# The folded weights' results go through the raw-weight ring, in stores of 512 KB

## The chip, the cores and the metric

The kernel runs on one core of a Trainium2 chip. A core has a matrix engine (TensorE, PE in the profile), a vector engine (VectorE, DVE), a scalar engine (ScalarE, ACT), GpSimd (POOL) and SyncE (SP), which here only issues DMAs. Each engine takes its instructions in order and waits on semaphores; DMAs are issued from the queues of SP, ACT and POOL. The metric is the time of one execution in microseconds (us), lower is better; a run's time is compared with that of the kernel before on the same chip.

## The reference

A decoder layer over 2048 tokens of width 1024: retention (4 heads) and a pooling mixer beside each other, an output projection, cross-attention into 256 memory tokens, a gated MLP with a short convolution, and a last norm, all in f32. What matters here is the part on the weights:

```python
y_pool = pool_mixer(u, pool_w[l], pool_scale[l])            # per group g: pooled_g @ pool_w[g] * scale
x = x + jnp.concatenate([y_ret, y_pool], axis=-1) @ w_out[l]
...
q = (h @ wq).reshape(B, S, XA_HEADS, XA_HEAD_DIM)
k, v = jnp.split(mem_n @ wkv, 2, axis=-1)
s = jnp.einsum('bshd,bmhd->bhsm', q, k) * (XA_HEAD_DIM ** -0.5)
p = jax.nn.softmax(s, axis=-1)
o = jnp.einsum('bhsm,bmhd->bshd', p, v).reshape(B, S, D_MODEL)
return o @ wo
```

The memory has only 256 rows, so the kernel multiplies weights by it once: M = wq k^T (for the scores straight from the hidden state), VW = v wo (for the output straight from the probabilities), and WP = pool_w w_out (pooled rows straight into the output projection). These are the folded weights.

## The kernel before

Every f32 matrix is split into a high and a low part (`split`, line 230: ACT copies the high part, DVE subtracts for the low part), and a product is three matmuls (`passes`, line 239, lines 241 to 243). `unit` (line 286) multiplies one 1024 x 128 block of a weight with 1024 tokens: 48 matmuls of 128x512 into two PSUM banks.

Raw weights come from memory into `R`, a ring of five places of 512 KB (`raws`, line 145). `new_raw` (line 245) takes the place that was given back first and gives it back at once, so places go around in the order in which the program takes them, whatever order the loads are issued in. A load waits for the last reader of its place. From `R` a unit's weights are split into `Q` (three pairs of halves), the rows of `wqT`, `wo` and `wout_p` into pieces of `G` (`row_pairs`, line 424).

`folded_weights` (line 361) is a generator; its steps are put between the units of the first 1024 tokens. First come the keys and values of the memory (16 steps). Then, from line 461 on, the part of this change:

- M: for each of four heads two row pairs of `wqT`, four PSUM banks of 12 matmuls (128x256) each; a bank is evacuated by ACT in two halves (line 473) and stored in `Md` (256 KB).
- VW: for each head two row pairs of `wo`, four banks of 6 matmuls (128x512), each evacuated by ACT (line 491) and stored in `VWd` (256 KB).
- WP: `poolT` and four row pairs of `wout_p`, eight banks of 3 matmuls, evacuated at line 512 and stored in `WPd`.

The evacuation goes into a temporary (`TT`, ten of 256 KB, shared with retention, pooling and the norms), and `keep` (line 432) issues the store on ACT's own DMA queue and gives the temporary back, to be written again when the store has landed.

The order of the program around it (line 1517): head 0 has its gate, q and k units, with one M step behind q and one behind k; head 1 the same; head 2 has two VW steps behind q and two behind k; head 3 two WP steps behind q and the rest behind k; then come four pool groups. Retention of a head runs in steps between the matmuls of the next units. The order in which each engine issues its instructions is made by a scheduler that works on its own estimate of times, so it may put instructions of neighbouring steps before one another, and it differs between the two kernels in this stage. Weight sums for the MLP (`weight_sums`, line 906) are made by copies on SP (line 916) and accumulating DMAs on POOL (lines 918 to 925) through the same time.

Of the kernel before, what the change touches and what calls it, by code (L numbers as in the profile page):

```python
# [11 lines left out]
AF = mybir.ActivationFunctionType  # L12
# [5 lines left out]
KT = D // P  # L18
SEQ = 2048
NMEM = 256  # L20
T = 1024
SUB = 512
# [97 lines left out]
def trunk(ctx, tc, xT, memT, pos, w_qkgu, w_v, wkv, wqT, wo, wout_r, wout_p, poolT, w_up, w_dn, vecs, consts, outT):  # L120
    nc = tc.nc
    pe, act, dve, pool, sp = nc.tensor, nc.scalar, nc.vector, nc.gpsimd, nc.sync
# [19 lines left out]
    TT = Arena(cp.tile([P, TEMPS * TW], F32, tag="T", name="T"), 0, TEMPS, TW)  # L142
# [9 lines left out]
    def vec(n):  # L152
        nonlocal o
        o += n
        return vc[:, o - n : o]

    mixg, xag, memg, ffng, fing = (vec(KT) for _ in range(5))
# [29 lines left out]
    t = TT.take()  # L187
# [5 lines left out]
    Md = drp.tile([2, KT, P, SUB], F32, tag="Md", name="Md")  # L193
    VWd = drp.tile([KT, P, KT, P], F32, tag="VWd", name="VWd")
    rope_d = drp.tile([2, P, SUB], F32, tag="rope_d", name="rope_d")
    WPd = drp.tile([KT, P, 4, P], F32, tag="WPd", name="WPd")

    def mmps():
        return mmp.tile([P, SUB], F32, tag="mm", name=nm("mm"))
# [30 lines left out]
    def split(src, hi, lo, g=None):  # L230

        if g is None:
            act.activation(hi, src, AF.Copy)  # L233
            tt(dve, lo, src, hi.bitcast(F32), ALU.subtract)
        else:
            act.activation(hi, src, AF.Identity, scale=g)
            stt(lo, src, g, hi.bitcast(F32), ALU.mult, ALU.subtract)

    def passes(ps, lhs, rhs, start, stop, more=False):
        (lh, ll), (rh, rl) = lhs, rhs  # L240
        pe.matmul(ps, lh, rh, start=start, stop=False, skip_group_check=more)  # L241
        pe.matmul(ps, lh, rl, start=False, stop=False, skip_group_check=more)  # L242
        pe.matmul(ps, ll, rh, start=False, stop=stop, skip_group_check=more)  # L243

    def new_raw():
        r = raws.take()
        r.free()
        return r.f
# [112 lines left out]
    def folded_weights():  # L361
# [20 lines left out]
        rn = smp.tile([P, 4], F32, tag="rnm", name="rnm", bufs=1)[:, :2]  # L382
# [17 lines left out]
        def project(n):  # L400

            if n < 2:
                hs = first[0] if n == 0 else pairs(first[1])
            elif n < KT and n % 2:

                z = Z.take()
                hs = pairs(load_tile(wkv[n], z))
                z.free()
            elif n % 2:
                zs = [TT.take() for _ in range(2)]  # L410
                for i in range(2):
                    sp.dma_start(zs[i].f[:, :SUB], wkv[n, :, 4 * i : 4 * i + 4].rearrange("p k n -> p (k n)"))
                hs = pairs([z.f[:, :SUB] for z in zs])
                for z in zs:
                    z.free()
            else:
                hs = pairs(load_tile(wkv[n]))
            ps = mmps()[:, :NMEM]
            for k in range(KT):
                w = [hs[k // 4][:, i, (k % 4) * P : (k % 4 + 1) * P] for i in range(2)]  # L420
                passes(ps, w, (mh[:, k], ml[:, k]), k == 0, k == KT - 1)
            return ps

        def row_pairs(src):
            raw = new_raw()
            sp.dma_start(raw, src)
            u = B.take(2)
            for i in range(2):
                split(raw[:, i * SUB : (i + 1) * SUB], u.r[:, i * SUB : (i + 1) * SUB], u.r[:, T + i * SUB : T + (i + 1) * SUB])
            return u  # L430

        def keep(dst, t, n):
            act.dma_start(dst, t.f[:, :SUB].rearrange("p (n c) -> p n c", n=n))
            t.free()

        def tiles4(d, nh, k):
            return d[4 * nh : 4 * nh + 4, :, k, :].rearrange("n p c -> p n c")

        kk = B.take(4)
        kp4 = kk.r.rearrange("p (n i m) -> p n i m", i=2, m=NMEM)  # L440
# [2 lines left out]
        for n in range(KT):  # L443
            ps = begun[n] if n < 2 else project(n)
            t = TT.take()
# [8 lines left out]
        for n in range(KT):  # L454
            ps = project(KT + n)
# [5 lines left out]
        for h in range(HEADS):  # L461
            dp = [row_pairs(wqT[(2 * h + dt) * P : (2 * h + dt + 1) * P, :]) for dt in range(2)]
            for k2 in range(KT // 2):
                ps = mmps()
                for j in range(2):
                    for dt in range(2):
                        k = 2 * k2 + j
                        w = [dp[dt].r[:, i * T + k * P : i * T + (k + 1) * P] for i in range(2)]
                        passes(ps[:, j * NMEM : (j + 1) * NMEM], w, (kp4[:, 2 * h + dt, 0], kp4[:, 2 * h + dt, 1]), dt == 0, dt == 1)
                t = TT.take()  # L470
                for j in range(2):
                    k = 2 * k2 + j
                    act.activation(t.f[:, j * NMEM : (j + 1) * NMEM], ps[:, j * NMEM : (j + 1) * NMEM], AF.Identity, scale=xag[:, k : k + 1])
                keep(Md[h // 2, 2 * k2 : 2 * k2 + 2, :, (h % 2) * NMEM : (h % 2 + 1) * NMEM].rearrange("k p m -> p k m"), t, 2)
            for u in dp:
                u.free()
            if h == HEADS - 1:
                kk.free()
            yield

        for h in range(HEADS):
            dp = [row_pairs(wo[(2 * h + dt) * P : (2 * h + dt + 1) * P, :]) for dt in range(2)]
            for mt in range(2):
                for nh in range(2):
                    ps = mmps()
                    for dt in range(2):
                        lh = [vp4[:, 2 * h + dt, i, mt * P : (mt + 1) * P] for i in range(2)]
                        w = [dp[dt].r[:, i * T + nh * SUB : i * T + (nh + 1) * SUB] for i in range(2)]
                        passes(ps, lh, w, dt == 0, dt == 1)
                    t = TT.take()  # L490
                    act.activation(t.f[:, :SUB], ps, AF.Identity, scale=rn[:, mt : mt + 1])
                    keep(tiles4(VWd, nh, 2 * h + mt), t, 4)
            for u in dp:
                u.free()
            if h == HEADS - 1:
                vv.free()
            yield
# [6 lines left out]
        split(raw[:, :SUB], pw.r[:, :SUB], pw.r[:, SUB:])  # L504
        for g in range(4):
            u = row_pairs(wout_p[g])
            for nh in range(2):
                ps = mmps()
                lh = [pw.r[:, i * SUB + g * P : i * SUB + (g + 1) * P] for i in range(2)]
                passes(ps, lh, [u.r[:, i * T + nh * SUB : i * T + (nh + 1) * SUB] for i in range(2)], True, True)  # L510
                t = TT.take()
                act.activation(t.f[:, :SUB], ps, AF.Copy)
                keep(tiles4(WPd, nh, g), t, 4)
            u.free()
            if g == 3:
                pw.free()
            yield
# [950 lines left out]
    def later_tiles(b, j, rb):  # L1468
# [11 lines left out]
        after(2, step)  # L1480

    todo = folded_weights()

    def folded(n):
# [14 lines left out]
    for b in range(NB):  # L1499
# [4 lines left out]
        rn, rb, last = normed  # L1504
# [119 lines left out]
    old, TT = TT, Places([], SUB)  # L1624
# [104 lines left out]
```

## Time and profile before

| | |
|---|---|
| median of 3 runs | 2493.02 us (2491.94 to 2494.43) |
| profiled execution | 2497.84 us, span 2495.7 us |
| TensorE busy | 2441.3 us (98%) |
| ACT busy | 1220.2 us (49%) |
| DVE busy | 1704.0 us (68%) |
| mean granted TensorE clock | 0.991 |
| stores of folded weights | 16 to Md, 16 to VWd, 8 to WPd, 256 KB each |
| first and last of them issued | 144.8 us and 337.4 us |

A row of waits reads: who waited, on whom, total us, times, longest. A row of the timeline: start, length, engine, line, operation, what it writes and reads. A row of windows: the stretch, its length, busy time and instruction count of TensorE, its weight loads, DVE, ACT and POOL, the granted TensorE clock (1.00 is full), the DMA engines' busy share, GB/s. A DMA row: what it writes and reads, the issuing queue, count, KB each, us from issue to landing.

### The profile page before, as it was taken

The page shows a single profiled execution, that of the slowest core. Times are in us where ns is not written, and L with a number is a line of the kernel's source. Part 1 is how long each engine was busy: PE and PEld are TensorE (multiplying, and loading weights), DVE is VectorE, ACT ScalarE, POOL GpSimd, SP SyncE. Part 2 cuts the span into 40 slices and gives each one's busy share as a digit, 9 for nine tenths or more (in the row PEclk, how much of TensorE's full clock was granted, in tenths as well). Part 3 has the DMA queues.
Part 4 walks back from the last instruction along what each step waited for, and adds up shares of the span by engine and source line. Part 5 has one row for each costly group of instructions (what it writes and reads, how often), then busy time and mean ns, then how long its engine had stood idle before and what let it go on. Part 6 is the DMA issues. An engine that isn't in the chain of part 4 may idle for free. (4 is left out here: it accounts for less than half of the span.)

```text
span 2495.7 us, 33069 instructions
## 1 busy us (share of the span) xinstructions
PE 2441.3 (98%) x11390; PEld 2039.3 (82%) x11390; DVE 1704.0 (68%) x2789; ACT 1220.2 (49%) x2171; POOL 374.2 (15%) x364
## 2 busy tenths in 40 slices
PE   6999999999999999999998999999999999999997
PEld 6888788888788888888887888888888887888885
DVE  8646576564636574575777776896677687877875
ACT  6333423443321223434654555675555576666663
POOL 1010111100111110030025130332113021000001
PEclk9999999999999999999999999999999999999998
DMA  9363889716766764365567565665556468768951
GB/s 317 91 169 110 232 193 244 230 46 208 223 136 151 153 160 152 101 247 199 175 203 250 182 195 158 206 225 172 157 164 214 132 217 300 244 190 282 340 166 68
DMA packets 257176, 474.27 MB, mean 190 GB/s; under 512 B 26864, under 2 KB 56176, under 8 KB 257008
## 3 DMA queue, kind: packets, MB, share of 16 engines
q1 hardware_dynamic: 212336, 408.18, 49.7%
q0 software_dynamic: 19584, 34.61, 9.1%
q10 hardware_dynamic: 25088, 29.37, 3.4%
q8 instruction: 89, 1.46, 0.2%
q14 instruction: 79, 0.65, 0.1%
HBM read 370.87 MB, written 170.39 MB: 217 GB/s over the span
## 5 line engine op out<-in xcount | busy, mean ns | idle before, releaser
L241 PE MATMUL mm<-G,Q 128*128 128x512 f32 (+1 forms) x1888 | 728.3, 386 | 16.1 <-ACT Q L233 10.5
L243 PE MATMUL mm<-G,Q 128*128 128x512 f32 (+1 forms) x1888 | 727.1, 386 | 4.5 <-DVE Q L216 4.5
L242 PE MATMUL mm<-G,Q 128*128 128x512 f32 (+1 forms) x1888 | 726.2, 385 | 0.0
L241 PE MATMUL mm<-G 128*128 128x512 f32 (+1 forms) x1380 | 531.5, 387 | 10.4 <-DVE Z L216 7.3
L243 PE MATMUL mm<-G 128*128 128x512 f32 (+1 forms) x1380 | 532.8, 387 | 2.3 <-DVE G L216 2.3
L242 PE MATMUL mm<-G 128*128 128x512 f32 (+1 forms) x1380 | 533.0, 386 | 0.0
L241 PEld LDWEIGHTS mm<-G,Q 128*128 128x128 f32 x1888 | 358.2, 190 | 84.2 <-ACT Q L233 11.2
L243 PEld LDWEIGHTS mm<-G,Q 128*128 128x128 f32 x1888 | 357.7, 190 | 73.6 <-DVE Q L216 5.4
L242 PEld LDWEIGHTS mm<-G,Q 128*128 128x128 f32 x1888 | 358.3, 190 | 68.0 <-DVE G L216 0.4
L241 PEld LDWEIGHTS mm<-G 128*128 128x128 f32 x1380 | 260.4, 189 | 64.6 <-DVE Z L216 6.3
L243 PEld LDWEIGHTS mm<-G 128*128 128x128 f32 x1380 | 260.6, 189 | 54.6 <-DVE G L216 2.8
L242 PEld LDWEIGHTS mm<-G 128*128 128x128 f32 x1380 | 260.8, 189 | 51.6
L225 DVE SCALAR_TENSOR_TENSOR Z<-Z,vecs 128x1024 f32<-128x1024 f32 x176 | 244.8, 1394 | 55.4 <-ACT Z L1070 50.7
L216 DVE TENSOR_TENSOR Q<-R,Q 128x512 fp32r<-128x512 f32 x235 | 176.0, 751 | 152.2 <-ACT Q L233 142.5
L1007 ACT ACTIVATE G<-R 128x512 fp32r<-128x512 f32 (+1 forms) x272 | 167.1, 615 | 228.7 <-PE mm L242 222.0
L216 DVE TENSOR_TENSOR G<-R,G 128x512 fp32r<-128x512 f32 (+1 forms) x268 | 197.0, 743 | 114.4 <-ACT G L1007 76.0
L216 DVE TENSOR_TENSOR Z<-Z,mm 128x512 f32<-128x512 f32 x284 | 193.6, 682 | 89.3 <-PE mm L243 88.9
L233 ACT ACTIVATE Q<-R 128x512 fp32r<-128x512 f32 x150 | 93.6, 628 | 246.2 <-PE mm L242 219.1
L216 DVE TENSOR_TENSOR G<-T,G 128x512 fp32r<-128x512 f32 (+1 forms) x201 | 135.0, 686 | 51.9 <-ACT G L956 38.4
L1007 ACT ACTIVATE Q<-R 128x512 fp32r<-128x512 f32 (+1 forms) x204 | 125.2, 614 | 76.3 <-PE mm L242 61.9
L1070 ACT ACTIVATE Z<-Z,vecs 128x1024 f32<-128x1024 f32 x88 | 109.3, 1242 | 52.4 <-DVE Z L216 50.8
L941 ACT ACTIVATE aux<-R 128x512 f32<-128x512 f32 (+1 forms) x184 | 105.4, 575 | 47.8 <-DVE Q L216 23.8
(217 smaller groups left out, 2647.7 us busy)
## 6 DMA issues: line engine op xcount, KB each, us to landing
R<-Ud SPq DMA_DIRECT2D x176, 256.0 KB, 2.8
T<-Gd SPq DMA_DIRECT2D x168, 256.0 KB, 4.2
R<-w_up SPq DMA_DIRECT2D x132, 256.0 KB, 3.1
Gd<-Z SPq DMA_DIRECT2D x110, 256.0 KB, 2.5
Ud<-w_up SPq DMA_DIRECT2D x88, 256.0 KB, 6.2
R<-w_qkgu SPq DMA_DIRECT2D x32, 512.0 KB, 4.5
R<-Dd SPq DMA_DIRECT2D x64, 256.0 KB, 4.2
Gd<-T SPq DMA_DIRECT2D x56, 256.0 KB, 3.1
```

Of the source, the lines that this page charges most:

```text
L216: return eng.tensor_tensor(out=out, in0=a, in1=b, op=op)
L225: dve.scalar_tensor_tensor(out=out, in0=a, scalar=s, in1=b, op0=op0, op1=op1)
L233: act.activation(hi, src, AF.Copy)
L241: pe.matmul(ps, lh, rh, start=start, stop=False, skip_group_check=more)
L242: pe.matmul(ps, lh, rl, start=False, stop=False, skip_group_check=more)
L243: pe.matmul(ps, ll, rh, start=False, stop=stop, skip_group_check=more)
L941: act.activation(t, x, AF.Copy)
L1007: act.activation(p2[:, 0, :w], self.raw[i].f[:, :w], AF.Copy)
L1070: act.activation(self.c[g].f, a[:, 2:], AF.Identity, bias=cb[:, f : f + 1], scale=cw[2][:, f : f + 1])
```

## The change

The results are evacuated into places of the ring `R` (`new_raw`), four M quarters or two halves of a VW or WP row to a place, and a store takes the whole place: 512 KB. There are 20 stores in place of 40, and no temporaries are taken. `keep` gives nothing back, since `new_raw` has done it.

```diff
         def keep(dst, t, n):
-            act.dma_start(dst, t.f[:, :SUB].rearrange("p (n c) -> p n c", n=n))
-            t.free()
-
-        def tiles4(d, nh, k):
-            return d[4 * nh : 4 * nh + 4, :, k, :].rearrange("n p c -> p n c")
+            act.dma_start(dst, t.rearrange("p (n c) -> p n c", n=n))
+
+        def column(d, k):
+            return d[:, :, k, :].rearrange("n p c -> p n c")
...
             for k2 in range(KT // 2):
                 ps = mmps()
+                if k2 % 2 == 0:
+                    t = new_raw()
...
-                t = TT.take()
                 for j in range(2):
                     k = 2 * k2 + j
-                    act.activation(t.f[:, j * NMEM : (j + 1) * NMEM], ps[:, j * NMEM : (j + 1) * NMEM], AF.Identity, scale=xag[:, k : k + 1])
-                keep(Md[h // 2, 2 * k2 : 2 * k2 + 2, :, (h % 2) * NMEM : (h % 2 + 1) * NMEM].rearrange("k p m -> p k m"), t, 2)
+                    act.activation(t[:, k % 4 * NMEM : (k % 4 + 1) * NMEM], ps[:, j * NMEM : (j + 1) * NMEM], AF.Identity, scale=xag[:, k : k + 1])
+                if k2 % 2:
+                    keep(Md[h // 2, 2 * k2 - 2 : 2 * k2 + 2, :, (h % 2) * NMEM : (h % 2 + 1) * NMEM].rearrange("k p m -> p k m"), t, 4)
...
             for mt in range(2):
+                t = new_raw()
                 for nh in range(2):
...
-                    t = TT.take()
-                    act.activation(t.f[:, :SUB], ps, AF.Identity, scale=rn[:, mt : mt + 1])
-                    keep(tiles4(VWd, nh, 2 * h + mt), t, 4)
+                    act.activation(t[:, nh * SUB : (nh + 1) * SUB], ps, AF.Identity, scale=rn[:, mt : mt + 1])
+                keep(column(VWd, 2 * h + mt), t, KT)
...
             u = row_pairs(wout_p[g])
+            t = new_raw()
             for nh in range(2):
...
-                t = TT.take()
-                act.activation(t.f[:, :SUB], ps, AF.Copy)
-                keep(tiles4(WPd, nh, g), t, 4)
+                act.activation(t[:, nh * SUB : (nh + 1) * SUB], ps, AF.Copy)
+            keep(column(WPd, g), t, KT)
```

## The prediction

> **What bounds the kernel now.** I read the page first, then TensorE's own waits in the stage that the change touches, then that stage in windows, then the DMAs.
>
> The page: span, busy time, and two DMA rows (KB each, median us from issue to landing).
>
> ```profile
> span 2495.7 us, 33069 instructions
> PE 2441.3 (98%) x11390; PEld 2039.3 (82%) x11390; DVE 1704.0 (68%) x2789; ACT 1220.2 (49%) x2171; POOL 374.2 (15%) x364
> R<-w_qkgu SPq DMA_DIRECT2D x32, 512.0 KB, 4.5
> ```
>
> TensorE is busy for 98% of the span, so time is won or lost only where TensorE stands still or runs at a lower clock. The folded weights lie between 145 us and 338 us. TensorE's waits from 100 to 350 us (total, times, longest), then ACT's and, last, the SP queue's:
>
> ```profile
> PE mm L241 <- ACT T L491: 2.3, 1, 2.3
> PE aux L750 <- ACT T L745: 0.9, 1, 0.9
> PE aux L778 <- DVE T L216: 0.5, 1, 0.5
> PE mm L241 <- ACT T L473: 0.5, 1, 0.5
> ...
> ACT T L491 <- DMA VWd<-T: 9.1, 2, 8.6
> ACT T L745 <- DMA Md<-T: 6.7, 1, 6.7
> ...
> SPq L306 <- DVE G L216: 58.0, 7, 36.1
> SPq L426 <- DVE Q L216: 31.2, 7, 14.3
> ```
>
> So 250 us hold only 4.2 us of TensorE waits. Two of the four have a temporary behind them: ACT stands for 8.6 us because the store that holds a temporary has not landed, and TensorE, out of PSUM banks, stands behind it for 2.3 us; and 0.9 us follow an ACT wait for an Md store. The SP rows say that a weight load goes out when its place in the ring is read out: the ring of five sets how early loads go.
>
> Windows around that wait and two others (columns: TensorE, weight load, DVE, ACT, POOL busy, granted clock, DMA share, GB/s):
>
> ```profile
> 276.60:279.20 2.60, 0.42 (x2) 0.00 (x0) 1.38 (x2) 0.60 (x2) 0.81 (x1) 1.00 0.09 19
> 279.80:283.20 3.40, 3.40 (x13) 2.91 (x12) 1.29 (x2) 2.51 (x5) 0.00 (x0) 0.50 1.06 184
> 2071.00:2075.00 4.00, 1.87 (x9) 1.26 (x8) 2.53 (x5) 2.85 (x7) 0.52 (x1) 1.00 1.02 371
> 2075.20:2078.60 3.40, 3.40 (x10) 2.63 (x9) 1.59 (x4) 1.41 (x3) 0.00 (x0) 0.50 1.02 356
> ```
>
> Each standstill of over 2 us is followed by 3.4 us at a granted clock of 0.50, so it costs half of that, 1.7 us, on top of itself.
>
> **The change, part by part.**
>
> *Half the stores.* 40 stores of 256 KB become 20 of 512 KB. Bytes and the length of the contiguous pieces stay as they were. 20 issues go from ACT's queue, at 0.37 us each (the timeline row below), 7.4 us. ACT is busy for 49% of the span and TensorE hides this; I count nothing. If ACT had no slack it would be a gain of that size at most. The 56 evacuations keep their number and shapes and write the ring in place of the temporaries: nothing.
>
> *No temporaries.* What waited for Md, VWd and WPd stores to hand back a temporary no longer does. On the path this is 2.3 us, its 1.7 us of half clock, and the 0.9 us: **-4.9 us**. Bounds: 0 if the same waits return on ring places, and -5.9 with the other two TensorE rows gone too.
>
> *20 more takes in the ring.* This is the other side. Places are taken in program order, five takes apart share a place. Beside 37 loads from the first head to the last pool group, 20 results now take a place each. A load that follows a result into its place must wait until that result was computed, evacuated, stored and landed. Going through the order of takes, most of these loads have a whole unit (48 matmuls) or two between the store and their use, and lose nothing: the rows of wqT and wo behind M tiles, wout_p behind V tiles, the last pool groups. Two have not, and both are unit loads for which before went out long ahead of use. With K2 the k-columns of head 2 and G3 the gate columns of head 3, the timeline of before (start, length) shows their loads, the first matmul of V0, of V1 and of K2 (the first to read Q), a store's issue, and the first matmul of G3:
>
> ```profile
> 231.96 0.33 SPq L306 DMA_DIRECT2D R<-w_qkgu  x1
> 242.64 0.33 SPq L306 DMA_DIRECT2D R<-w_qkgu  x1
> 249.86 0.40 PE L241 MATMUL mm<-G 128*128 128x512 f32 x1
> 252.17 0.37 ACTq L433 DMA_DIRECT2D VWd<-T  x1
> 255.34 0.39 PE L241 MATMUL mm<-G 128*128 128x512 f32 x1
> 261.90 0.39 PE L241 MATMUL mm<-G,Q 128*128 128x512 f32 x1
> ...
> 288.56 0.39 PE L241 MATMUL mm<-G,Q 128*128 128x512 f32 x1
> ```
>
> Before, K2's load leaves 30 us and G3's 46 us ahead of use. In the changed kernel K2 takes the place of V0's second result, and G3 that of V2's second. Between the end of V0 and the start of K2 TensorE has only V1 and four small matmuls: 261.90 - 255.34 = 6.6 us. Between the end of V2 and G3 it has V3, as long as V0 (255.34 - 249.86 = 5.5 us), and in the built order 18 small matmuls of retention, which at 0.61 us for four are 2.7 us: 8.2 us in all. In that time must pass: the evacuation, the store, the load and the first high part. Their rows: evacuation and high part (mean ns after the bar), the only 512 KB store from ACT, the results' stores, the landing of w_qkgu (min/median/max), and four rows of the crowded stretch 255 to 266 us:
>
> ```profile
> L491 ACT ACTIVATE T<-mm,rnm 128x512 f32<-128x512 f32 x16 | 10.9, 686 | 13.8 <-DMA VWd<-T 9.1 <-PE mm L243 3.1 <-PE aux L778 1.1
> L233 ACT ACTIVATE Q<-R 128x512 fp32r<-128x512 f32 x25 | 15.7, 630 | 56.4 <-PE mm L242 53.3 <-DMA R<-w_qkgu 3.1
> 243.76 0.61 PE L750 MATMUL aux<-Z,T 128*128 128x128 f32 x4
> Xd<-Z ACTq DMA_DIRECT2D x16, 512.0 KB, 4.2
> VWd<-T ACTq DMA_DIRECT2D x16, 256.0 KB, 5.1
> Md<-T ACTq DMA_DIRECT2D x16, 256.0 KB, 2.9
> DMA to landing us min/median/max: 3.5/4.5/12.0
> ...
> VWd<-T ACTq DMA_DIRECT2D x6, 256.0 KB, 7.4
> Ud<-w_up SPq DMA_DIRECT2D x4, 256.0 KB, 6.7
> R<-wout_p SPq DMA_DIRECT2D x2, 512.0 KB, 9.1
> R<-w_qkgu SPq DMA_DIRECT2D x1, 512.0 KB, 4.8
> ```
>
> K2: evacuation 0.69, one high part ahead of it on ACT 0.63, store 4.2 (the row of the same size and queue), load 4.5, high part 0.63: 10.7 us against 6.6, so TensorE stands for **+4.1 us**. From below: a store as quick as Md's 2.9, a load at 3.5, nothing ahead on ACT: 7.7 us, +1.1. From above: 7.4 and 4.8 of the crowded stretch: 14.2, +7.6. The low part, due next, is covered: the built order puts 16 matmuls of V2 there. This standstill brings its half clock: **+1.7 us**.
>
> Behind K2's load on the SP queue stand the pool weights, wo's last row pair, the q-columns of head 3, four weight-sum copies, the k-columns of head 3, then G3. The copies go out some 10 us behind K2's landing and their POOL accumulations follow when V2's last result is stored. That is the mixture of the crowded stretch (four Ud copies, VWd stores, a unit load), so I take its rows: 0.69 + 7.4 + 4.8 + 0.63 = 13.5 us against 8.2, **+5.3 us**, and again **+1.7 us**. From below: 0.69 + 2.9 + 3.5 + 0.63 = 7.7, nothing; from above a load at 9.1 and a store at the 12.0 that is the slowest landing in these rows: 22.4, +14.2. Waiting on ACT for G3's high part, behind it in order, are the row pairs of wout_p, the other half of q and the retention squares; they delay work that TensorE needs some 20 us later. I leave that at 0, up to +5.
>
> A row-pair load of head 2 (wqT) now follows an M store too, and DVE's retention copies stand behind its low part; TensorE has about 11 us of work there against a chain of the same length. 0, up to +2.
>
> Sum: 4.1 + 1.7 + 5.3 + 1.7 - 4.9 = **+7.9 us**. Against the profiled execution's own 2497.8 us (span 2495.7) this is 2505.7; that execution lies 4.8 us above the median of the runs, so the forecast for the median is 2493.0 + 7.9 = **2501 us**.
>
> By the Trainium skill (TensorE: Matmul & The Clock Gate, HAM oscillation) the clock falls back when an idle stretch passes a window of about 3.4 us. The trace above differs: 2.6 us were enough. Waits of 4.1 and 5.3 us in one piece pay by either; by the page they would pay nothing beyond themselves if they came in pieces below its window.
>
> The Trainium skill (DMA: Bandwidth & Descriptors, Rules for kernel authors) tells to coalesce small transfers, for a fixed cost of about 2.0 us per DMA; as an estimate from that page 20 fewer stores would save 40 us of such cost. No TensorE row above waits for that cost itself, only for places; by that rule alone the time would fall, if it lay on the path: the first rival.
>
> **The rivals.** 0.2%, 5 us, is about what a measurement of this kernel tells from no change.
>
> *Faster: the larger store is as good as free.* Both chains fit into their 6.6 and 8.2 us. The temporaries' -4.9 stays alone: 2488 us. For it: TensorE's one long wait in this stage is a temporary's. Against: K2's chain from the lowest rows is 7.7 us already; it decides when store and load together take less than 5.3 us, and the quickest rows are 2.9 + 3.5.
>
> *No change: short waits.* K2 at +1.1 to +2, under what brings half clock, G3 at 0 to +3, less 4.9: 2491 to 2495, say 2493. For it: the stage's quiet DMAs land in 2.9 and 3.5 us, and the change takes the temporaries' stores out of the crowd. Against: medians, not minima, are the rule here.
>
> *Much slower: G3 meets the accumulations in full.* Store 12, load 9.1 as wout_p's: +14.2 in place of +5.3, so 2493.0 + 16.8 = 2510 us. For it: in the crowded stretch a store made ACT wait for 8.6 us. Against: G3's own kind of load landed in 4.8 there.
>
> *No half clock.* Both waits come, each in two or three pieces of under 2 us (high part, low part, the next half), and the clock stays: 2493.0 + 4.1 + 5.3 - 4.9 = 2497.5. Against it: it is one load that comes late, and both its high parts with it. The page's longer window would make this case wider.
>
> **How the numbers follow.** Forecast 0.45; much slower 0.20; no change 0.22; no half clock 0.05; faster 0.08. Slower by over 0.2%: 0.45 + 0.20 = 0.65. Within: 0.22 + 0.05 = 0.27. Faster: 0.08. The range goes from 2491 (the short waits' lower end) to 2513 (the much slower case with 3 us of the unknowns behind G3); outside lie the faster case and a little of the far end. The forecast's own range, from K2's and G3's middle bounds, is 2497 to 2507.
>
> **What would show it.** In the profile after: a TensorE wait of 3 to 6 us at the first matmul of K2 and a second at G3, ended by ACT Q L233, itself waiting for R<-w_qkgu; in the SP queue's waits w_qkgu loads waiting for VWd<-R; 3.4 us at 0.50 behind each; the wait of L491 for VWd gone from TensorE's rows; 20 stores of 512 KB landing in 4 to 8 us; the page's TensorE busy time unchanged within a few us. Wrong it would be if these loads still went out long before use, if the stores landed in under 3 us, or if the time were lost elsewhere, as at the k-columns of head 3 behind ACT's queue.

## The result and the profile after

The changed kernel takes **2501.32 us** in the median of 6 runs (2498.17 to 2507.82); the kernel before, on the same chip, takes 2493.01 us in the median of 6 (2490.11 to 2495.33). The ratio is 1.004, with a 95% interval from 1.003 to 1.005: slower, by about 8 us. The forecast was 2501.

The page after (span, busy time), and the DMA rows of the new stores (count, KB each, median us from issue to landing):

```profile
span 2498.8 us, 33008 instructions
PE 2441.6 (98%) x11390; PEld 2039.5 (82%) x11390; DVE 1704.7 (68%) x2789; ACT 1221.7 (49%) x2171; POOL 374.2 (15%) x364
Md<-R ACTq DMA_DIRECT2D x8, 512.0 KB, 4.2
VWd<-R ACTq DMA_DIRECT2D x8, 512.0 KB, 5.0
WPd<-R ACTq DMA_DIRECT2D x4, 512.0 KB, 6.5
```

The profiled execution took 2500.54 us. No engine has more work to do: TensorE is busy for 2441.6 us against 2441.3. The loss is in standing still. The waits of TensorE, then two rows of ACT's and two of the SP queue's, from 100 to 360 us:

```profile
PE mm L241 <- ACT Q L233: 8.1, 2, 4.4
PE aux L751 <- ACT T L746: 0.8, 1, 0.8
...
ACT Q L233 <- DMA R<-w_qkgu: 6.2, 2, 5.5
...
SPq L306 <- DMA VWd<-R: 6.6, 2, 4.1
SPq L426 <- DMA VWd<-R: 2.9, 1, 2.9
```

TensorE waits twice, 8.1 us together, for the high part of a unit's weight; ACT, which makes it, waits for the load of that weight; and the SP queue, which issues the load, waits for a store of `VWd` out of a ring place. The wait of L491 on a temporary has gone.

The timeline of both chains (start, length, and in brackets the wait ahead and what ended it). First K2, the k-columns of head 2, then G3, the gate columns of head 3:

```profile
254.49 0.37 ACTq L433 DMA_DIRECT2D VWd<-R  x1
258.04 0.33 SPq L306 DMA_DIRECT2D R<-w_qkgu  x1
258.97 0.40 PE L243 MATMUL mm<-G 128*128 128x512 f32 x1
263.10 1.15 ACT L233 ACTIVATE Q<-R 128x512 fp32r<-128x512 f32 x2 [0.67 <-DMA R<-w_qkgu]
263.78 0.50 PE L241 MATMUL mm<-G,Q 128*128 128x512 f32 x1 [4.42 <-ACT Q L233]
...
282.81 0.37 ACTq L433 DMA_DIRECT2D VWd<-R  x1
288.19 0.33 SPq L306 DMA_DIRECT2D R<-w_qkgu  x1
289.64 1.16 PE L751 MATMUL aux<-Z,T 128*128 128x128 f32 x8 [0.78 <-ACT T L746]
...
295.10 1.15 ACT L233 ACTIVATE Q<-R 128x512 fp32r<-128x512 f32 x2 [5.51 <-DMA R<-w_qkgu]
295.78 0.79 PE L241 MATMUL mm<-G,Q 128*128 128x512 f32 x1 [3.64 <-ACT Q L233]
```

K2: the store is issued at 254.49; the load behind it goes out at 258.04, when the store has landed, and lands 5 us later; the high part follows at 263.10 and TensorE's first matmul at 263.78, 4.42 us late. Before, this load went out at 231.96. G3 is the same chain one head later (store 282.81, load 288.19, high part 295.10), 3.64 us late, with a wait of 0.78 us for retention shortly ahead. The windows around both (columns as above; the last three are granted clock, DMA share, GB/s):

```profile
259.40:263.80 4.40, 0.02 (x1) 0.02 (x1) 2.32 (x5) 2.94 (x6) 0.00 (x0) 1.00 1.02 325
264.70:268.10 3.40, 3.40 (x10) 2.63 (x9) 1.05 (x2) 0.00 (x0) 0.00 (x0) 0.50 0.60 185
291.90:295.30 3.40, 0.24 (x3) 0.05 (x1) 0.00 (x0) 0.20 (x1) 0.00 (x0) 1.00 1.08 345
295.40:298.80 3.40, 3.02 (x7) 2.44 (x8) 2.81 (x6) 2.00 (x4) 0.00 (x0) 0.50 0.36 101
```

Each standstill is followed by 3.4 us at half clock, of which TensorE is busy for 3.40 and 3.02 us: 1.7 and 1.5 us lost. In this execution the two places cost 4.42 + 1.7 + 3.64 + 0.78 + 1.5 = 12.0 us.

### The profile page after: what moved, and what is told of

It reads as the page before. It is cut to its first block, busy times and chain, and to the rows that moved or that the text cites. A ratio compares the mean times of both kernels' runs of the same rounds, so it can differ in the third digit from the quotient of the medians.

```text
span 2498.8 us, 33008 instructions
## 1 busy us (share of the span) xinstructions
PE 2441.6 (98%) x11390; PEld 2039.5 (82%) x11390; DVE 1704.7 (68%) x2789; ACT 1221.7 (49%) x2171; POOL 374.2 (15%) x364
```

## The experiments

The theory: the loss is the late loads of K2 and G3, which now stand behind results in the ring. The first rival: it is the larger stores (they land later, and crowd the DMA engines). The second: it is the ring as such, at other loads than these two. A third question is whether the temporaries' waits, which the prediction counted as a gain of 4.9 us, were a cost at all.

### Which takes cost: VW alone, or M and WP alone

In the first kernel VW goes back to temporaries, and M and WP stay in the ring; the second is the kernel before with VW alone in the ring.

```diff
# the changed kernel, VW loop
-                t = new_raw()
...
-                    act.activation(t[:, nh * SUB : (nh + 1) * SUB], ps, AF.Identity, scale=rn[:, mt : mt + 1])
-                keep(column(VWd, 2 * h + mt), t, KT)
+                    t = TT.take()
+                    act.activation(t.f[:, :SUB], ps, AF.Identity, scale=rn[:, mt : mt + 1])
+                    keep_t(tiles4(VWd, nh, 2 * h + mt), t, 4)
```

> Only VW goes back to temporaries and stores of 256 KB; M and WP stay in the ring. Theory (K2's and G3's loads come late because each follows a VW result into its place): TensorE's two waits on ACT Q L233 (8.1 us together) are gone with their two half-clock stretches (3.4 us); the wait on a temporary's VWd store (2.3 us and 1.7 us of half clock) may come back. 2488 to 2494 us. Rival (the loss lies in 20 more takes anywhere in the ring, M and WP as much as VW): over half of the 8 us stays, 2497 us or more.

> Only VW goes through the ring in stores of 512 KB; M and WP are as in the kernel before. Theory: the whole loss is here: K2 and G3 late again, two TensorE waits on ACT Q L233 of 3 to 5 us each, 2498 to 2504 us. Rival (M and WP carry it): 2493 us or less.

Without VW in the ring: 2491.22 us (12 runs; ratio 0.9994, 0.9985 to 1.0003), no change. With VW alone: 2503.27 us (1.0041, 1.0029 to 1.0053), the whole loss. TensorE's waits of the second kernel from 100 to 360 us:

```profile
PE mm L241 <- ACT Q L233: 4.6, 1, 4.6
PE aux L756 <- ACT T L751: 2.1, 1, 2.1
```

K2's wait is there. At the place of G3 it is a retention matmul that waits for 2.1 us, with the half clock behind it. The 12 stores of M and WP, with their places in the ring, cost nothing that can be measured.

### The two loads early

In the first of these kernels the places of K2 and G3 are taken before the VW results that they followed, and given back at once, as everywhere in the ring.

```diff
...
+        raw = load_tile(w_qkgu[4 + h]) if early else None
         ...
-        unit(load_tile(w_qkgu[4 + h]), xpair, rope_evac(1))
+        unit(raw if early else load_tile(w_qkgu[4 + h]), xpair, rope_evac(1))
+        if early and h + 1 < HEADS:
+            gate_ahead.append(load_tile(w_qkgu[9 + h]))
```

> The changed kernel, with two takes moved: the places of K2 (k-columns of head 2) and G3 (gate columns of head 3) are taken, and their loads written, ahead of the VW steps that they followed. Same 20 stores of 512 KB, same bytes. Theory: both waits go, nothing waits for a temporary, so the gain of 4.9 us that the prediction counted stands alone: 2486 to 2491 us, faster than the kernel before. Rival (512 KB stores crowd the DMAs or land late whatever the places): the loss stays, 2498 us or more.

2494.73 us (11 runs; 1.0006, 0.9997 to 1.0014). The K2 and G3 waits are gone and smaller ones of 2.6, 1.9 and 1.0 us stand elsewhere. But as the places were given back at once they were handed out again before they were read, so the k-columns of head 2 and the gate of head 3 were computed from other data. The work is the same, yet some waits are not those of a kernel that holds the places. So it was done again with `raws.take()`, and the place given back only when the weight has been split:

```diff
+    def held(w):
+        room = raws.take()
+        load_tile(w, room)
+        return room
+
+    def ready(room):
+        hs = pairs(room.f)
+        room.free()
+        return hs
...
+        room = held(w_qkgu[4 + h]) if ahead[0] else None
...
+        if ahead[1]:
+            gate_ahead.append(held(w_qkgu[9 + h]))
```

> As the run with the two early takes, but the places of K2 and G3 stay held until they are read, so the VW steps go around four places and all products are those of the reference. Theory (the two late loads are the loss): no TensorE wait on ACT Q L233 at K2 or G3, no wait for a temporary: 2486 to 2492 us. Rival (with four places the VW results and row pairs wait for one another, and the wait only moves to the folded matmuls): TensorE waits on ACT R L493 or at V rows, 2495 us or more.

> Only K2's place is held ahead; G3 still follows V2's second result. Theory: K2's 4.4 us and its half clock go, G3's 3.7 us and its half clock stay: 2494 to 2498 us, halfway between the changed kernel and the one with both held. Rival (one wait hides the other: with K2 on time G3 is later by as much): 2500 us or more.

With both held: 2493.22 us (11 runs; 0.9997, 0.9988 to 1.0006). With K2's alone: 2496.16 us (11 runs; 1.0010, 1.0002 to 1.0019). The SP queue of the kernel with both held shows K2's load out early, and TensorE's waits from 100 to 360 us are nearly nothing:

```profile
231.05 0.33 SPq L306 DMA_DIRECT2D R<-w_qkgu  x1
...
PE aux L781 <- DVE T L225: 1.2, 1, 1.2
PE aux L781 <- DVE T L771: 0.7, 1, 0.7
```

ACT still waits there for 6.8 us for places of `VWd` stores, since while a place is held VW goes round with fewer; TensorE does not feel it. With K2's alone the G3 wait stays, at 5.2 us:

```profile
PE mm L241 <- ACT Q L233: 5.2, 1, 5.2
```

This settles the theory: the ring, the 20 large stores and the missing temporaries are all still there, and with two loads moved ahead the loss is gone. In run medians, K2's load is worth 2501.32 - 2493.01 = 8.3 less 2496.16 - 2493.88 = 2.3, that is 6.0 us, and G3's 2496.16 - 2493.22 = 2.9 us. Each of these carries 2 us or more of uncertainty, by the intervals.

### The size of the store

The first kernel has the 512 KB stores, but out of two adjacent temporaries; the second has VW in the ring, each half stored by itself.

```diff
# first: stores of 512 KB from temporaries (likewise for M and WP)
-                t = new_raw()
+                t = TT.take(2)
...
-            act.dma_start(dst, t.rearrange("p (n c) -> p n c", n=n))
+            act.dma_start(dst, t.f[:, :T].rearrange("p (n c) -> p n c", n=n))
+            t.free()
```

```diff
# second: VW in the ring, two stores of 256 KB
-                keep(column(VWd, 2 * h + mt), t, KT)
+                    keep(column(VWd[4 * nh : 4 * nh + 4], 2 * h + mt), t[:, nh * SUB : (nh + 1) * SUB], 4)
```

> 20 stores of 512 KB, but out of two neighbouring temporaries each, none out of the ring. Theory: no load follows a result, so no wait at K2 or G3; ACT waits for temporaries as in the kernel before or longer, since two come free at a time: 2490 to 2497 us. Rival (the store's size costs the time): TensorE still loses about 8 us, 2499 us or more.

> The changed kernel with the VW results still in the ring, but each half stored by itself as soon as it is evacuated (16 stores of 256 KB for VW, in place of 8 of 512 KB). Theory: a place is free again when its last half has landed, and that half is quicker to land than a whole place (2.3 to 3.5 against 3.5 to 4.6 us in quiet stretches): K2's wait shrinks by about 1 us, G3's by 1 to 2, 2497 to 2500 us. Rival (it is the store's size that costs): back to 2493 us. Rival (the ring alone, size without effect): 2501 us.

Large stores from temporaries: 2495.7 us (11 runs; 1.0009, 1.0000 to 1.0017). So the size is not the loss, and no gain from 20 stores fewer shows. Its profile has a wait of its own in this stage:

```profile
PE aux L780 <- DVE T L216: 3.6, 1, 3.6
```

Behind it come 6.8 us at half clock, with TensorE busy for 6.02 of them, so 3.0 us lost. VectorE was busy for 3.44 of the 3.60 us from 260.0 to 263.6, so TensorE stood here for other work of VectorE's and not for a store. Small stores from the ring: 2507.15 us (6 runs; 1.0052, 1.0040 to 1.0063), where I had expected less than the changed kernel. Its interval overlaps that of the changed kernel (1.003 to 1.005), so that it is the slower of the two is likely and not shown. Its K2 chain, and its TensorE waits:

```profile
255.07 0.37 ACTq L433 DMA_DIRECT2D VWd<-R  x1
257.64 0.33 SPq L306 DMA_DIRECT2D R<-w_qkgu  x1
263.27 1.15 ACT L233 ACTIVATE Q<-R 128x512 fp32r<-128x512 f32 x2 [0.99 <-DMA R<-w_qkgu]
...
PE mm L241 <- ACT Q L233: 10.6, 2, 6.6
```

The last half is issued at 255.07 and has landed by 257.64, 2.6 us later, where the whole place took 3.5. So the load goes out 0.4 us earlier (257.64 against 258.04). It takes longer, though: the high part comes at 263.27 against 263.10. What the store gave, the load took. The longer wait, 6.6 us, is G3's. Its load goes out at 287.60 us, 0.6 us before the changed kernel's, but the built order has only 12 small matmuls of retention between V2 and G3, where the changed kernel has 32; the other 20 come later. Another part of its longer time lies in a later stage: from 440 to 700 us TensorE waits for 4.9 us, against 1.8 us in the changed kernel. Why is open.

### A ring of four

```diff
-    raws = Places([(R, j * T) for j in range(5)], T)
+    raws = Places([(R, j * T) for j in range(4)], T)
```

> The changed kernel with four of the ring's five places used in this stage: one cost doubled. Theory: every load follows a result or a load one take sooner, so more unit loads go out late: two or more TensorE waits on ACT Q L233 or on row pairs beside or in place of the two, 2505 us or more. Rival (places do not matter, the larger stores do): 2501 us as with five.

2511.28 us (6 runs; 1.0071, 1.0055 to 1.0086): the time came as expected, the place did not. Two TensorE rows of this kernel, the first from 380 to 620 us, the second from 100 to 360:

```profile
PE mm L243 <- DVE Q L216: 6.3, 1, 6.3
...
PE aux L766 <- DVE T L756: 2.4, 2, 2.1
```

With one place fewer for the whole program, another stage loses more (6.3 us at one place) and the K2 and G3 waits are not those of the changed kernel. It is no test of the theory.

### The same kernels again

The kernel before (twice), the kernel with VW in temporaries, and the changed kernel, one execution each, all on one chip and profiled, the kernels as they were:

> The kernel before, looked at again: its profiled execution lay 4.8 us over its median, and the kernel with VW alone on temporaries 7.5 us over its own. Theory (the wait on a temporary's VWd store comes in some executions only): an execution near 2493 us has no TensorE wait on ACT T L491 and no half clock near 280 us, one near 2497 us has both. Rival (it is there each time; the excess is from later stages): the wait of 2 to 3 us shows at any time of the execution.

> As the look before it, a second one: same theory and rival, same numbers.

> VW alone on temporaries, looked at again. Theory: near its median of 2491 us the wait on ACT T L499 is under 1 us; with the wait of 3 us the time is 2495 us or more. Rival: 3 us of wait at 2491 us.

> The changed kernel, looked at again. Theory: K2's and G3's waits hang on a chain of store and load that is there each time, so both come again with 3 to 6 us each and a half-clock stretch behind each, 2499 to 2505 us. Rival (they come in some executions only): one or both under 2 us.

2489.42, 2489.73, 2494.62 and 2502.53 us, with a further run of the kernel before at 2493.61 us. In both executions of before, the L491 wait on ACT is still there, as is the store that it waits for; TensorE, which stood for 2.3 us behind it in the first profile, does not stand behind it at all. Both lie 3 to 4 us under the median of before, so they do not say whether an execution at 2493 us has the wait. The first of them: ACT's row from 100 to 360 us, TensorE's only row from 255 to 300 us, and the two windows which the prediction showed of before:

```profile
ACT T L491 <- DMA VWd<-T: 4.1, 1, 4.1
...
PE aux L778 <- DVE T L216: 0.5, 1, 0.5
...
276.60:279.20 2.60, 2.60 (x17) 2.23 (x15) 0.69 (x1) 1.99 (x4) 0.81 (x1) 1.00 1.05 239
279.80:283.20 3.40, 3.40 (x17) 2.79 (x16) 0.39 (x1) 2.00 (x3) 0.00 (x0) 1.00 0.97 269
```

ACT's wait is 4.1 us long here (5.7 in the second) in place of 8.6. TensorE goes on with matmuls in the meantime, so the wait is hidden. The kernel with VW in temporaries does the same: 3.1 us of TensorE wait with half clock behind it in its first profile (of an execution of 2498.69 us), none in the second. Between the two its time fell by 4.1 us, about what the wait and its half clock took (3.1 + 1.6). The second still took 2494.62 us, more than this kernel's median of 2491.22. Half clock between 1349 and 1391 us is in every one of the 14 profiles, for 3.4 to 10.2 us; here it lasts for 10.2 us, behind a TensorE wait of 2.5 us (6.8 us in this kernel's first profile):

```profile
1352.00:1362.20 10.20, 6.59 (x15) 4.75 (x16) 9.09 (x9) 4.83 (x7) 6.38 (x5) 0.52 0.86 278
```

A little under half of the 6.59 us, some 3.2, is lost. So losses elsewhere change from one execution to the next as well, and the time without the wait in this stage need not be a low one; that part of what I expected did not come.

The changed kernel's waits, in contrast, come again, with more half clock (TensorE's longest wait row from 100 to 360 us, and two windows):

```profile
PE mm L241 <- ACT Q L233: 8.2, 2, 4.2
...
261.40:268.20 6.80, 4.71 (x11) 3.74 (x12) 3.33 (x6) 2.09 (x4) 0.00 (x0) 0.50 0.80 243
295.60:302.40 6.80, 5.96 (x16) 4.90 (x17) 3.96 (x9) 3.14 (x6) 0.00 (x0) 0.50 0.44 139
```

With the wait of 0.8 us ahead of G3, which comes again too, the two places cost 8.2 + 0.8 + 2.4 + 3.0 = 14.4 us in this execution, where the first had 12.0.

## Why the prediction was right, step by step

**The takes in the ring: right, down to the two places.** Of all the loads that now follow a result, the two named are the ones that come late, by the chain foretold. K2 was put at +4.1 us of wait and measured 4.42. Of its parts, store and load were put at 4.2 + 4.5 = 8.7 us; they took 3.5 and 5.0 (254.49 to 258.04, and 5.0 to landing). With half clock, 5.8 us were foretold; the runs with and without K2's late load differ by 6.0 in their medians.

**G3: right place, a wait 0.9 us shorter than put.** It was put at +5.3 us and came at 3.64 + 0.78 = 4.4, and the half clock at 1.7 came at 1.5. From the store's issue to the high part 295.10 - 282.81 = 12.3 us went by, for which 7.4 + 4.8 = 12.2 stood in the sum; only the shares differ, 5.4 for the store and 6.9 for the load. What was off is the work ahead. From V2's last matmul (282.05) to G3's first (295.78) are 13.7 us, near the 13.5 of the sum, but TensorE had 9.3 us to do in them and not 8.2: 32 small matmuls of retention ran there, where 18 had been counted. Two other profiles put the place at about the 7.0 of the sum, with half clock: 4.0 + 0.8 + 3.0 = 7.8 us in the changed kernel's second execution, and 5.2 + 2.2 = 7.4 us in the kernel with K2's place alone held (the 2.2 is half of the 4.39 us for which TensorE is busy at half clock, 285.1 to 291.9 us). In the medians of runs it is worth only 2.9 us. The kernel with both loads held stands for 1.2 + 0.7 us of its own a little later, which is a part of this; the rest may be the uncertainty of the 2.9, and no run decides it.

**No temporaries: the gain that did not show.** The step "On the path this is 2.3 us, its 1.7 us of half clock, and the 0.9 us: -4.9 us" was not borne out. The three rows were in the profile of before, but that was an execution at 2497.84 us, 4.8 us over the median, and the wait was one of the reasons why it was slow: it and its half clock are 4.0 of the 8.4 us between this execution and the one of 2489.4. The two further executions, at 2489.4 and 2489.7 us, have no such wait. Nor does a gain show in runs: the kernel with both loads held has no temporaries, no late loads, and is level with before (0.9997, 0.9988 to 1.0006). By that interval at most 3 us of gain are left, net of the 1.9 us for which that kernel stands. How often an execution of before has the wait is not known; of three profiles one has it. The prediction took its durations from one execution and added the sum to the median of others; that is sound only for terms that every execution has, and this term is not one of them.

**The sum.** By the medians: 6.0 (K2) + 2.9 (G3) - 0.7 (the rest, 2493.22 - 2493.88) = 8.2 us, against a sum of 5.8 + 7.0 - 4.9 = 7.9. The three parts are differences along one chain of kernels, so they add up to the whole by construction and are no check of it. Read so, G3 was some 4 us too dear and the temporaries' gain some 4 us too large, and the two cancelled. By the profiles the two places cost 12.0 and 14.4 us, around the 5.8 + 7.0 = 12.8 of the sum. Then some 4 us of the 12 must be lost in the median execution of before and not in the changed kernel. The executions of 2489 us do not lose them, and no execution of before at 2493 us was profiled, so this stays open. By either reading the places and the mechanism were right, and that the forecast hit 2501 within a microsecond was luck.

**Half the stores, at nothing: right.** 20 stores fewer are worth nothing measurable: the kernel with held loads is level (0.9997), and the one with large stores from temporaries (1.0009) is no faster either. The rule of the Trainium skill (DMA: Bandwidth & Descriptors, Rules for kernel authors) that small transfers be coalesced calls transfers under 64 KB mostly overhead; the stores here had 256 KB, and no run shows a gain.

**The unknowns left at 0.** No wait shows at wqT's row pairs of head 2, nor at work behind G3 on ACT's queue: TensorE's list after has three waits in all in the stage, and they are those above.

**The rivals.** "Faster" falls: both chains were longer than their cover. "No change" falls for the same reason, and so does "no half clock": the loads came late in one piece. "Much slower" falls in its mechanism, since G3's load landed within 7 us and did not meet the accumulations in full. Only the highest run of the changed kernel, 2507.82 us, comes near its 2510.

## What to carry to other kernels

Where places of a ring go round in program order, a result that takes a place puts the next load of that place behind its computing, its evacuation, its store and the store's landing: go through the takes and compare that chain with the matmul work left before the load's use, load by load. Here 2 of some 37 loads were short of cover, by about 4 us each, and moving these two ahead repaired it. And before a wait in one profiled execution is counted as a gain, see how that execution stands to the median; one that is slow may be slow by just that wait, so a second profile is worth having.

## What the runs showed of the hardware

**Half clock comes in pieces of 3.4 us.** Behind a wait there are one to three of them; the 10.2 us shown above are three. Only at the end of the program does it last longer (in before from 2478.0 us to the end). The changed kernel had 3.4 and 3.4 in one execution, 6.8 and 6.8 in another, behind nearly equal waits (4.4 and 3.6; 4.2 and 4.0). What it takes is half of TensorE's busy time in it, so 1.5 to 3.0 us a place (3.02 / 2 and 5.96 / 2), and executions of one kernel differ by that.

**No fixed length of wait brings it; where the wait falls on a grid of 3.41 us does.** In before 2.3 us did (the 2.6 us in the prediction are the window around them, and its "each standstill of over 2 us" holds for the two that it shows); in the kernel with VW alone in the ring 2.1 us did; in the kernel with early loads a wait of 2.6 us did not. In each of the 14 profiles, all stretches at half clock start whole steps of 3.41 us apart. In the changed kernel they start at 32.56, 264.67, 295.39, 674.27, 1367.17 and 2479.92 us, which is 68, 9, 111, 203 and 326 steps from one to the next. The grid lies elsewhere in each execution. What tells the two waits apart is how busy TensorE is in one step. Two steps of VW alone (its wait is from 289.7 to 291.8):

```profile
289.20:292.60 3.40, 1.30 (x11) 1.06 (x10) 1.89 (x3) 2.30 (x4) 0.00 (x0) 1.00 1.12 266
292.60:296.00 3.40, 3.40 (x17) 3.32 (x16) 0.90 (x3) 1.15 (x2) 0.00 (x0) 0.50 1.05 358
```

and two of early loads (its wait is from 304.4 to 307.0):

```profile
302.90:306.30 3.40, 1.55 (x7) 0.94 (x5) 2.41 (x4) 2.48 (x12) 0.00 (x0) 1.00 0.73 142
306.30:309.70 3.40, 2.66 (x16) 2.38 (x17) 2.24 (x9) 2.36 (x6) 0.00 (x0) 1.00 0.22 83
```

The first wait lies within one step, which leaves TensorE busy for 0.38 of it; the second is spread over two, with 0.46 and 0.78. Counted over all 14 profiles from the first full clock on, each of the 51 steps at full clock with a busy share under 0.44 was followed by half clock, 7 of the 14 between 0.44 and 0.52 were, and none above 0.52 was. Left out of this count are the stretch from 655 to 690 us and the program's end from 2460 us on; there half clock came behind busier steps as well, up to 0.92, and why is open. As an estimate from the 0.44, 1.9 us of standstill in one step (0.56 of 3.41) bring half clock. By the same estimate a wait of 1.9 to 3.8 us brings it or not by where it falls, and a longer one each time. The window of about 3.4 us in the Trainium skill (TensorE: Matmul & The Clock Gate, HAM oscillation) agrees with the step. As the idle time that must pass first it is too long by these runs.

**A store of half the size freed its place 0.9 us sooner** (2.6 against 3.5 us, one place in one profile each), and the load behind it took 0.6 us longer (5.6 against 5.1 us until the high part starts).
